# ScalarE reads a shared PSUM bank first, and the planner keeps accesses of one bank apart

## The chip, the cores and the metric

The kernel runs on one core of a Trainium2 chip. Five engines work on it side by side, each through a queue of its own, in order: TensorE (PE, matrix products into PSUM), VectorE (DVE), ScalarE (ACT), GpSimd (POOL) and SyncE (SP), which issues the DMA transfers. PSUM has eight banks of 512 fp32 values for each of 128 partitions; here each bank is one tile. The metric is the device time of one launch in microseconds.

## The reference

Two decoder layers are computed for 512 prompt tokens and 8 x 8 sample tokens (576 in all), model width 1024. Per layer:

```
h = rmsnorm(x); z = h @ w_in                      # rq rk rv rz, aq ak av az, iq ik iw, gr ga
rq, rk = rope(rq), rope(rk)                       # 4 heads of 128: rotary over the whole head
o_r = group_norm(retention(rq, rk, rv, state))    # 4 heads
score = sum_h relu(iq_h . ik) * iw_h              # indexer, 4 heads of 64
o_a = softmax attention of aq over the top-k keys by score (8 query heads, 2 key heads)
m = sigmoid(gr) * ((o_r * silu(rz)) @ w_o_ret) + sigmoid(ga) * ((o_a * silu(az)) @ w_o_att)
x = x + m @ w_out;  x = x + sigmoid(x @ w_ple_gate) * (p @ w_ple_proj)
```

All is fp32. The outputs are the tokens of both sets, the new keys, values and indexer keys, and the retention states.

## The kernel before

The work of a layer is written as some dozens of generators, each of which yields the instructions of one strand: a projection, the evacuation of one PSUM bank, the attention of one pair of heads, the retention of one head. Products are exact to fp32 by splitting each operand in a high and a low fp32r part (`hi`, `lo`; `whi`, `wlo` for weights, `xh`, `xl` for the tokens) and adding three matmuls.

What sets the order of the instructions in the engines' queues is a planner that runs while the program is built (class `Streams`). It keeps a clock for each engine and a log of accesses. For the next instruction of each strand `_ready` finds the time from which it may run: the end of each logged access that overlaps it in partitions **and columns**, where one of the two writes, plus a hop between engines (`HOP`), and a second, safer time with a margin (`MARGIN`, 1.0 for TensorE). `go` takes the strand whose instruction can start first by the safer time, appends that instruction to its engine's queue for good, and advances the clock. All instructions are recorded at line 299 of the kernel (`op.fn(*op.a, **op.k)`), so every row of the profile has that line, and the tiles tell what it is. The semaphores come from the framework, after the planner has fixed the order.

The eight banks are `pm` (three, the projections), `tq` (scores), `ta` (transposes), `oT` (attention output), `tr` and `acc` (retention). A strand takes a bank with `Get`, and gives it back with `K.put` when its last reader has been planned.

Four places read one bank with two engines, and the diff touches them:

- `ropeT` (line 1091): evacuates half of a rotary head from `pm` (32 halves in the program). VectorE multiplies it by the cosine (`d`, in the rows `xl<-pm,rot`), ScalarE copies the two partition halves crosswise into `tb` (`tb<-pm`, 64x288), VectorE multiplies `tb` by the sine and adds.
- `cross_split` (line 743): splits transposed queries from `ta` into high and low parts (`qs<-ta`, `iqs<-ta`), first for partitions 0 to 63, then for 64 to 127.
- `collect` (line 966): adds the crosswise halves of an attention output from `oT`.
- `ret_s` (line 1189): the sample side of a retention head. TensorE writes the sample scores (`tr<-xl 64x64`) and the transposed keys (`tr<-cst,xl 64x128`) into one `tr` bank; VectorE masks the scores (`xh<-tr,cst 64x64`), ScalarE takes the high part of the keys twice (`iqs<-tr`), VectorE the low part twice. Then TensorE writes the head's output into `acc` (`acc<-xh 32x128`, then `acc<-s,xl`).

The prompt side of a head (`ret_p`, line 1142) uses the same two banks: scores into `tr` (masked by `xh<-tr,cst 128x512`), the key transposes into `tr` (`tr<-cst,xl 128x128`, four), the output into `acc`, from which `group_norm` (line 1123) reads statistics with VectorE and then four blocks of columns with ScalarE (`xh<-acc,gs`), and the transposes of the result into `tr` (`tr<-cst,xh 128x128`).

A layer's projections come in the order of `PLAN`: keys, indexer queries, retention values, attention gates `az`, then for each of four heads `rq`, `rk`, `rz`, with the attention queries `aq` between them, then 16 gate units (`gr`, `ga`), which only fill TensorE beside the rest of the attention, then the merge (`pm<-oh,whi`, which needs all strands before it), the output projection and the gates of the layer's end.

Of the kernel before, what the change touches and what calls it, by code (L numbers as in the profile page):

```python
# [23 lines left out]
NS = 64  # L24
# [81 lines left out]
class Op:  # L106
    __slots__ = ("eng", "fn", "a", "k", "name", "outs", "ins", "dur", "form")

    def __init__(self, eng, fn, name, a, k):
        self.eng, self.fn, self.name, self.a, self.k = eng, fn, name, a, k  # L110
        aps = [x for x in list(a) + list(k.values()) if isinstance(x, bass.AP)]
        out = k.get("out", a[0] if a else None)
        acc = k.get("accum_out")
        self.outs = [_box(x) for x in (out, acc) if x is not None]
        self.form = (_val(a[1].partition_size) > 64, min(2, _free(a[1]) - 1 >> 5)) if eng == "PE" else None
        self.ins = [_box(x) for x in aps if x is not out and x is not acc]
        self.dur = _duration(eng, name, out, aps, a, k)
        if eng in ("DVE", "ACT") and len(self.ins) and self.outs[0][1] != self.ins[0][1]:
            self.dur += 0.12
# [78 lines left out]
class Streams:  # L198
# [7 lines left out]
    def __init__(self):  # L206
# [5 lines left out]
        self.count = 0  # L212
        self.form = None

    def spawn(self, gen, prio):
# [39 lines left out]
    def _ready(self, op):  # L255
        t = safe = 0.0
        for boxes, w in ((op.ins, False), (op.outs, True)):
            for name, p0, p1, c0, c1 in boxes:
                for e in self.log.get(name, ()):
                    if (w or e[6]) and e[0] < p1 and p0 < e[1] and e[2] < c1 and c0 < e[3]:  # L260
# [5 lines left out]
                        if r > safe:  # L266
                            safe = r
        return t, safe

    def _note(self, op, end):  # L270
        low = min(self.clock["PE"], self.clock["DVE"], self.clock["ACT"]) - 5.0
        for boxes, w in ((op.ins, False), (op.outs, True)):
# [41 lines left out]
def tile_hybrid_decoder(ctx: ExitStack, tc: tile.TileContext, A, O):  # L314
# [253 lines left out]
    def layer(l, xh, xl, kxb):  # L568
# [174 lines left out]
        def cross_split(dst, ps):  # L743
            d = dst.rearrange("p (a b) t -> p a b t", b=2)
            yield S.activation(d[0:64, :, 0, :], ps[0:64], AF.Copy)
            yield V.tensor_tensor(d[64:128, :, 0, :], ps[0:64], d[0:64, :, 0, :].bitcast(FT), OP.subtract)
            yield S.activation(d[64:128, :, 1, :], ps[64:128], AF.Copy)
            yield V.tensor_tensor(d[0:64, :, 1, :], ps[64:128], d[64:128, :, 1, :].bitcast(FT), OP.subtract)
# [217 lines left out]
        def collect(j, u, oT, done):  # L966
            yield done
            t = yield Get(T2)
            o = t[:, :256]
            for kv in range(2):  # L970
                mine, other = slice(kv * 64, kv * 64 + 64), slice(64 - kv * 64, 128 - kv * 64)
                c = slice(kv * 256, (kv + 1) * 256)
                yield S.activation(o[mine], oT[other, c], AF.Copy)
                yield V.tensor_tensor(o[mine], oT[mine, c], o[mine], OP.add)
            K.put(BANK["oT"], oT)
# [115 lines left out]
        def ropeT(dst, ev, free):  # L1091
            def evac(ps, cs):
# [4 lines left out]
                d = dst[:, cs]  # L1097
                yield V.tensor_tensor(d, ps[:, :TH], cosr[:, cs], OP.mult)
                yield S.activation(tb[0:64], ps[64:128, :TH], AF.Copy)
                yield S.activation(tb[64:128], ps[0:64, :TH], AF.Copy)  # L1100
                K.put(BANK["pm"], ps)
                yield V.tensor_tensor(tb, tb, sinr[:, cs], OP.mult)
# [86 lines left out]
        def ret_s(h, t):  # L1189
# [15 lines left out]
            yield V.memset(ins[:NS, NS:96], 0.0)  # L1205
            yield V.tensor_tensor(ins[:NS, :NS], b[:NS, :NS], con("blk", NS), OP.mult)
            yield S.activation(kh[:NS], b[:NS, 128:256], AF.Copy, scale=g8)
            yield S.activation(kh[NS:], b[:NS, 128:256], AF.Copy, scale=g8)
            for rows in (slice(0, NS), slice(NS, 128)):
                yield V.scalar_tensor_tensor(kl[rows], b[:NS, 128:256], g8, kh[:NS].bitcast(FT), op0=OP.mult,  # L1210
# [415 lines left out]
```

## Time and profile before

| | us |
|---|---|
| timed runs, median (lowest to highest) of 3 | 1113.51 (1112.26 to 1114.78) |
| profiled execution, device time | 1115.49 |
| its span, first to last instruction | 1113.7 |
| TensorE busy in the span | 1084.8 (97%) |
| VectorE / ScalarE busy | 759.1 (68%) / 525.2 (47%) |
[...]

A busy TensorE is read with care: matmuls overlap, and their ends are modelled. Its speed is better read from the distance of their starts, and its losses from the idle time that the waits name. An engine's idle time costs something only where another engine waits for what it does next.

### The profile page before, as it was taken

To read this page: it belongs to the slowest core of one execution; us is meant where nothing else is said; L and a number is where in the kernel's file an instruction comes from. 1 tells how busy PE (TensorE), PEld (TensorE's weight loads), DVE (VectorE), ACT (ScalarE), POOL (GpSimd) and SP (SyncE) were. 2 spreads that over 40 slices of the span, in tenths; PEclk is the share of its full clock that TensorE was granted. 3 is DMA by queue.
4 is the path that set the end of the run, shared out by engine and by line. 5 is a ranking of instruction groups with operands and counts; after the bars stand their busy time and mean duration, and the time that the engine had idled before them with its cause. 6 is when DMAs were issued, how large, how long until landed. Compare 5 with 4: busy or idle time off the path is not lost.

```text
span 1113.7 us, 21594 instructions
## 1 busy us (share of the span) xinstructions
PE 1084.8 (97%) x8426; PEld 1049.9 (94%) x8426; DVE 759.1 (68%) x1979; ACT 525.2 (47%) x1116; POOL 57.4 (5%) x68
## 2 busy tenths in 40 slices
PE   8999899999999999999999998999999999999998
PEld 7989898989999999999999998988989999999998
DVE  6799999976555476534658999998755554764343
ACT  6743264666465343234546333555654655232431
POOL 0100012100000000000010001120000000000000
PEclk9999999999999999999999999999999999999999
DMA  6532221324323364522335221222242233553231
GB/s 199 160 109 74 87 68 69 99 76 127 111 89 118 103 200 156 182 89 97 108 116 163 79 76 58 88 87 98 74 130 102 90 112 131 183 198 121 94 114 48
DMA packets 53112, 124.80 MB, mean 112 GB/s; under 512 B 7442, under 2 KB 19602, under 8 KB 53010
## 3 DMA queue, kind: packets, MB, share of 16 engines
q1 hardware_dynamic: 53010, 123.42, 33.7%
q8 instruction: 66, 1.08, 0.4%
q14 instruction: 36, 0.29, 0.1%
HBM read 103.05 MB, written 20.35 MB: 111 GB/s over the span
## 4 chain that ended last, share of the span: by engine, by line
PE 63%; DVE 28%; ACT 3%; issue 2%; DMA 1%; SPq 1%; POOL 0%; DVEq 0%; ACTq 0%
PE pm L299 53%; DVE xl L299 7%; DVE sm L299 5%; DVE wlo L299 5%; PE oT L299 3%; PE tq L299 3%; PE acc L299 2%; DVE misc L299 2%; DVE silz L299 2%; PE ta L299 2%; PE tr L299 1%; DVE t2k L299 1%; DVE iqs L299 1%; DVE tb L299 1%; DVE qs L299 1%
## 5 line engine op out<-in xcount | busy, mean ns | idle before, releaser
L299 PE MATMUL pm<-xh,whi 128*128 128x288 f32 x1536 | 458.2, 298 | 0.0
L299 PE MATMUL pm<-xl,whi 128*128 128x288 f32 x1536 | 457.1, 298 | 0.0
L299 PE MATMUL pm<-xh,wlo 128*128 128x288 f32 x1536 | 456.8, 297 | 0.0
L299 PEld LDWEIGHTS pm<-xl,whi 128*128 128x128 f32 x1536 | 290.4, 189 | 1.6 <-issue 0.5
L299 PEld LDWEIGHTS pm<-xh,whi 128*128 128x128 f32 x1536 | 290.1, 189 | 0.9
L299 PEld LDWEIGHTS pm<-xh,wlo 128*128 128x128 f32 x1536 | 290.0, 189 | 0.8
L299 ACT ACTIVATE whi<-wst 128x1024 fp32r<-128x1024 f32 (+4 forms) x148 | 150.1, 1016 | 200.3 <-PE pm L299 128.6
L299 DVE TENSOR_TENSOR wlo<-wst,whi 128x1024 fp32r<-128x1024 f32 (+4 forms) x148 | 172.8, 1169 | 82.0 <-ACT whi L299 81.6
L299 PE MATMUL pm<-wlo,xh 128*128 128x256 f32 (+2 forms) x416 | 117.5, 290 | 1.9 <-DVE wlo L299 1.9
L299 PE MATMUL pm<-whi,xh 128*128 128x256 f32 (+2 forms) x416 | 118.2, 291 | 0.0
L299 PE MATMUL pm<-whi,xl 128*128 128x256 f32 (+2 forms) x320 | 93.0, 291 | 0.0
L299 PEld LDWEIGHTS pm<-wlo,xh 128*128 128x128 f32 x416 | 80.1, 193 | 3.5 <-DVE wlo L299 2.4
L299 PEld LDWEIGHTS pm<-whi,xh 128*128 128x128 f32 x416 | 80.1, 193 | 0.7 <-issue 0.4
L299 PE MATMUL pm<-oh,whi 128*128 128x288 f32 x240 | 70.9, 296 | 0.0
L299 PE MATMUL pm<-oh,wlo 128*128 128x288 f32 x240 | 70.9, 295 | 0.0
L299 PE MATMUL pm<-ol,whi 128*128 128x288 f32 x240 | 70.8, 295 | 0.0
L299 ACT ACTIVATE t2k<-t2k,sm 128x256 f32<-128x256 f32 (+3 forms) x102 | 58.7, 583 | 25.2 <-DVE sm L299 21.0
L299 PEld LDWEIGHTS pm<-whi,xl 128*128 128x128 f32 x320 | 61.6, 193 | 0.5 <-issue 0.4
L299 DVE TENSOR_TENSOR misc<-pm,R 128x288 f32<-128x288 f32 x64 | 29.1, 454 | 41.9 <-PE pm L299 41.5
L299 DVE MAX8 sm<-xl 128x8 f32<-128x256 f32 (+2 forms) x96 | 52.4, 549 | 0.8
L299 DVE MATCH_REPLACE8 xl<-sm,xl 128x256 f32<-128x256 f32 (+2 forms) x96 | 51.7, 540 | 0.0
L299 DVE TENSOR_TENSOR ptl<-ta,pth 128x512 fp32r<-128x512 f32 (+1 forms) x48 | 28.7, 598 | 29.8 <-ACT pth L299 29.6
(257 smaller groups left out, 1711.7 us busy)
## 6 DMA issues: line engine op xcount, KB each, us to landing
wst<-in_wa SPq DMA_DIRECT2D x96, 512.0 KB, 3.5
wst<-in_wb SPq DMA_DIRECT2D x16, 512.0 KB, 3.9
wst<-in_wo SPq DMA_DIRECT2D x16, 512.0 KB, 4.0
zgr<-misc SPq DMA_DIRECT2D x16, 288.0 KB, 2.0
zga<-misc SPq DMA_DIRECT2D x16, 288.0 KB, 2.1
misc<-zgr SPq DMA_DIRECT2D x16, 288.0 KB, 2.8
misc<-zga SPq DMA_DIRECT2D x16, 288.0 KB, 4.4
s<-in_ckv SPq DMA_DIRECT2D x32, 128.0 KB, 3.2
```

The costliest lines, as they stand in the source:

```text
L299: op.fn(*op.a, **op.k)
```

## The change

The planner gets a second rule. Each instruction carries the set of PSUM banks that it touches (`banks`), and for each bank the planner notes when each engine's last planned access ends. An instruction may then be planned only after the accesses of all *other* engines to its banks, whichever columns they have, and whether they read or write; the hop between ScalarE and VectorE, which the table does not have, is 0.15. The four places above are written in another order: ScalarE's reads first, then VectorE's.

```diff
--- before.py
+++ after.py
@@ -104,7 +104,7 @@
 
 
 class Op:
-    __slots__ = ("eng", "fn", "a", "k", "name", "outs", "ins", "dur", "form")
+    __slots__ = ("eng", "fn", "a", "k", "name", "outs", "ins", "dur", "form", "banks")
 
     def __init__(self, eng, fn, name, a, k):
         self.eng, self.fn, self.name, self.a, self.k = eng, fn, name, a, k
@@ -112,6 +112,7 @@
         out = k.get("out", a[0] if a else None)
         acc = k.get("accum_out")
         self.outs = [_box(x) for x in (out, acc) if x is not None]
+        self.banks = {x.tensor.name for x in aps if x.space == PSUM}
         self.form = (_val(a[1].partition_size) > 64, min(2, _free(a[1]) - 1 >> 5)) if eng == "PE" else None
         self.ins = [_box(x) for x in aps if x is not out and x is not acc]
         self.dur = _duration(eng, name, out, aps, a, k)
@@ -211,6 +212,7 @@
         self.run = []
         self.count = 0
         self.form = None
+        self.bank = {}
 
     def spawn(self, gen, prio):
         self.count += 1
@@ -265,9 +267,17 @@
                             r += MARGIN.get(op.eng, 0.0)
                         if r > safe:
                             safe = r
+        for name in op.banks:
+            for eng, end in self.bank.get(name, {}).items():
+                if eng != op.eng:
+                    r = end + self.HOP.get((eng, op.eng), 0.15)
+                    t = max(t, r)
+                    safe = max(safe, r + MARGIN.get(op.eng, 0.0))
         return t, safe
 
     def _note(self, op, end):
+        for name in op.banks:
+            self.bank.setdefault(name, {})[op.eng] = end
         low = min(self.clock["PE"], self.clock["DVE"], self.clock["ACT"]) - 5.0
         for boxes, w in ((op.ins, False), (op.outs, True)):
             for name, p0, p1, c0, c1 in boxes:
@@ -743,8 +753,8 @@
         def cross_split(dst, ps):
             d = dst.rearrange("p (a b) t -> p a b t", b=2)
             yield S.activation(d[0:64, :, 0, :], ps[0:64], AF.Copy)
+            yield S.activation(d[64:128, :, 1, :], ps[64:128], AF.Copy)
             yield V.tensor_tensor(d[64:128, :, 0, :], ps[0:64], d[0:64, :, 0, :].bitcast(FT), OP.subtract)
-            yield S.activation(d[64:128, :, 1, :], ps[64:128], AF.Copy)
             yield V.tensor_tensor(d[0:64, :, 1, :], ps[64:128], d[64:128, :, 1, :].bitcast(FT), OP.subtract)
 
         iqt = {}
@@ -967,11 +977,11 @@
             yield done
             t = yield Get(T2)
             o = t[:, :256]
+            mine = [slice(kv * 64, kv * 64 + 64) for kv in range(2)]
             for kv in range(2):
-                mine, other = slice(kv * 64, kv * 64 + 64), slice(64 - kv * 64, 128 - kv * 64)
-                c = slice(kv * 256, (kv + 1) * 256)
-                yield S.activation(o[mine], oT[other, c], AF.Copy)
-                yield V.tensor_tensor(o[mine], oT[mine, c], o[mine], OP.add)
+                yield S.activation(o[mine[kv]], oT[mine[1 - kv], kv * 256:(kv + 1) * 256], AF.Copy)
+            for kv in range(2):
+                yield V.tensor_tensor(o[mine[kv]], oT[mine[kv], kv * 256:(kv + 1) * 256], o[mine[kv]], OP.add)
             K.put(BANK["oT"], oT)
             yield e_az
             z = silz[1][:, 2 * u:2 * u + 2, j * 128:(j + 1) * 128]
@@ -1095,9 +1105,9 @@
                     yield free
                 tb = yield Get(TB)
                 d = dst[:, cs]
-                yield V.tensor_tensor(d, ps[:, :TH], cosr[:, cs], OP.mult)
                 yield S.activation(tb[0:64], ps[64:128, :TH], AF.Copy)
                 yield S.activation(tb[64:128], ps[0:64, :TH], AF.Copy)
+                yield V.tensor_tensor(d, ps[:, :TH], cosr[:, cs], OP.mult)
                 K.put(BANK["pm"], ps)
                 yield V.tensor_tensor(tb, tb, sinr[:, cs], OP.mult)
                 yield V.tensor_tensor(d, d, tb, OP.add)
@@ -1203,9 +1213,9 @@
             ks = yield Get(IQS)
             kh, kl, vh = ks[:, 0], ks[:, 1], ks[:, 2]
             yield V.memset(ins[:NS, NS:96], 0.0)
-            yield V.tensor_tensor(ins[:NS, :NS], b[:NS, :NS], con("blk", NS), OP.mult)
             yield S.activation(kh[:NS], b[:NS, 128:256], AF.Copy, scale=g8)
             yield S.activation(kh[NS:], b[:NS, 128:256], AF.Copy, scale=g8)
+            yield V.tensor_tensor(ins[:NS, :NS], b[:NS, :NS], con("blk", NS), OP.mult)
             for rows in (slice(0, NS), slice(NS, 128)):
                 yield V.scalar_tensor_tensor(kl[rows], b[:NS, 128:256], g8, kh[:NS].bitcast(FT), op0=OP.mult,
                                              op1=OP.subtract)
```

The planner's rule shows in the order of the queues; three places follow, first as they were, then as they are. Names are output tile, then input tiles; a number behind an underscore is the buffer. The line at which the planner records is 309 now.

VectorE, the second and third rotary half of the first head's queries and keys in layer one. `xl<-pm,rot` is the product with the cosine, `tb<-tb,rot` that with the sine. Before:

```order
L299 TENSOR_TENSOR xl<-pm_69,rot 128x288 [waits PE_49]
L299 MATCH_REPLACE xl<-sm_417,xl 128x384 [waits DVE_49]
L299 MAX sm_412<-xl 128x8 [waits DVE_49]
L299 TENSOR_TENSOR wlo_125<-wst_120,whi_122 128x1024 [waits DMAHW7_49,Activation_49]
L299 TENSOR_TENSOR tb_434<-tb_434,rot 128x288 [waits Activation_49]
L299 MAX sm_413<-xl 128x8 [waits DVE_49]
L299 TENSOR_TENSOR xl<-xl,tb_434 128x288 [waits DVE_49]
L299 TENSOR_TENSOR xl<-pm_68,rot 128x288 [waits PE_49]
L299 TENSOR_TENSOR tb_433<-tb_433,rot 128x288 [waits Activation_49]
```

After:

```order
L309 MATCH_REPLACE xl<-sm_412,xl 128x384 [waits DVE_49]
L309 MAX sm_417<-xl 128x8 [waits DVE_49]
L309 TENSOR_TENSOR wlo_125<-wst_120,whi_122 128x1024 [waits DMAHW7_49,PE_49,Activation_49]
L309 TENSOR_TENSOR xl<-pm_69,rot 128x288 [waits Activation_49]
L309 TENSOR_TENSOR tb_434<-tb_434,rot 128x288
L309 MAX sm_414<-xl 128x8 [waits DVE_49]
L309 TENSOR_TENSOR xl<-xl,tb_434 128x288 [waits DVE_49]
L309 MATCH_REPLACE xl<-sm_414,xl 128x384 [waits DVE_49]
L309 TENSOR_TENSOR xl<-pm_68,rot 128x288 [waits PE_49,Activation_49]
L309 TENSOR_TENSOR tb_433<-tb_433,rot 128x288
```

The sine product stands right behind the cosine product, and the wait for ScalarE has moved from the one to the other.

TensorE, the first head of layer two, from the end of the projection that runs beside it. `tr_74<-cst,xl 128x128` are the four key transposes of the prompt side, `acc_75<-xh` and `acc_75<-s` the sample output. Before:

```order
L299 MATMUL pm_70<-wlo_125,xh 128x256
L299 MATMUL tr_74<-cst,xl 128x128 [waits DVE_49]
L299 MATMUL pm_70<-whi_122,xh 128x256
L299 MATMUL pm_70<-whi_122,xl 128x256
L299 MATMUL acc_75<-xh 32x128 x8
L299 MATMUL acc_75<-s_6216,xl 32x128 [waits DMAHW2_49]
L299 MATMUL ta_72<-cst,misc 128x128 x2
L299 MATMUL acc_75<-s_6216,xl 32x128 x7
L299 MATMUL tr_74<-cst,xl 128x128 x3
```

After:

```order
L309 MATMUL pm_70<-whi_122,xh 128x256
L309 MATMUL acc_75<-xh 32x128 [waits DVE_49]
L309 MATMUL acc_75<-xh 32x128 x7
L309 MATMUL acc_75<-s_6216,xl 32x128 [waits DMAHW2_49]
L309 MATMUL acc_75<-s_6216,xl 32x128 x2
L309 MATMUL ta_72<-cst,misc 128x128 [waits DVE_49]
L309 MATMUL ta_72<-cst,misc 128x128
L309 MATMUL acc_75<-s_6216,xl 32x128 x5
L309 MATMUL tr_74<-cst,xl 128x128 x4
```

The four transposes came in two parts, one ahead of the sample output and three behind; now all four stand behind it. Between the sample scores and the first transpose there were 23 rows, and now there are 38.

TensorE, the third head of layer one: `acc_75<-xh` is the first writer of `acc` after the group norm of the prompt side, `tr_74<-cst,xh` are the transposes of the normalised prompt output, `oT` is attention. Before:

```order
L299 MATMUL ta_72<-cst,misc 128x64 [waits DVE_49]
L299 MATMUL ta_72<-cst,misc 128x64
L299 MATMUL oT_73<-ptl_425,vhl 128x256
L299 MATMUL oT_73<-pth_424,vhl 128x256
L299 MATMUL oT_73<-ptl_425,vhl 128x256
L299 MATMUL acc_75<-xh 32x128 [waits Activation_49]
L299 MATMUL acc_75<-xh 32x128 x3
L299 MATMUL tr_74<-cst,xh 128x128 [waits DVE_49]
L299 MATMUL acc_75<-xh 32x128 x4
```

After:

```order
L309 MATMUL pm_69<-xh,whi_121 128x288
L309 MATMUL pm_69<-xl,whi_121 128x288
L309 MATMUL acc_75<-xh 32x128 [waits DVE_49,Activation_49]
L309 MATMUL acc_75<-xh 32x128 x7
L309 MATMUL acc_75<-s_430,xl 32x128 [waits DMAHW4_49]
L309 MATMUL acc_75<-s_430,xl 32x128 x7
L309 MATMUL oT_73<-pth_424,vhl 128x256 [waits Activation_49]
L309 MATMUL tr_74<-cst,xh 128x128 [waits DVE_49]
L309 MATMUL tr_74<-cst,xh 128x128 x3
```

The writer of `acc` has moved behind more projection matmuls (from 24 to 43 rows behind the sample scores of the head), and the transposes into `tr` behind the whole sample output.

## Rows read from the trace of the kernel before

**Rows 1.** The page: busy us, share of the span, instructions, by engine.
```profile
PE 1084.8 (97%) x8426; PEld 1049.9 (94%) x8426; DVE 759.1 (68%) x1979; ACT 525.2 (47%) x1116; POOL 57.4 (5%) x68
```

**Rows 2.** The chain that ended last, its longest pieces: start us, us, what.
```profile
399.19 159.22 PE pm L299 x1200
...
950.18 159.23 PE pm L299 x1200
```

**Rows 3.** Busy time by stage: stage, its length, engines' busy us, PEclk, DMA.
```profile
125.00:160.00 35.00, 31.69 (x257) 29.97 (x256) 33.81 (x118) 17.30 (x41) 5.96 (x6) 0.95 0.25 89
...
645.00:690.00 45.00, 40.45 (x314) 38.15 (x313) 42.51 (x122) 14.80 (x30) 2.02 (x2) 0.96 0.21 71
```

**Rows 4.** Waits of TensorE: us in total, times, longest us.
```profile
PE acc L299 <- ACT xh L299: 5.1, 7, 1.3
PE tr L299 <- DVE xh L299: 3.9, 2, 3.1
PE tr L299 <- DVE iqs L299: 3.6, 4, 2.1
```

**Rows 5.** Timeline around 777 us: start us, us, engine, operation [idle before].
```profile
774.77 0.44 ACT L299 ACTIVATE xh<-acc,gs 128x128 f32<-128x128 f32 x1
...
775.68 0.46 ACT L299 ACTIVATE xh<-acc,gs 128x128 f32<-128x128 f32 x1
...
776.24 0.79 ACT L299 ACTIVATE xh<-acc,gs 128x128 f32<-128x128 f32 x2
...
777.08 0.42 PE L299 MATMUL acc<-xh 64*32 64x128 f32 x8 [1.30 <-ACT xh L299]
```

**Rows 6.** Timeline of TensorE, five other users of the two banks.
```profile
180.19 0.30 PE L299 MATMUL tr<-cst,xh 128*128 128x128 f32 x1 [0.94 <-DVE iqs L299]
...
227.79 0.42 PE L299 MATMUL acc<-xh 64*32 64x128 f32 x8 [1.00 <-ACT xh L299]
...
684.39 0.33 PE L299 MATMUL tr<-cst,xl 128*128 128x128 f32 x1 [2.09 <-DVE iqs L299]
...
736.58 0.42 PE L299 MATMUL acc<-xh 64*32 64x128 f32 x8 [0.84 <-ACT xh L299]
...
812.87 0.31 PE L299 MATMUL acc<-xh 64*32 64x128 f32 x4 [0.89 <-ACT xh L299]
```

**Rows 7.** Busy time by stage, three stretches of 3.42 us with PEclk near 0.5.
```profile
228.86:232.28 3.42, 3.42 (x24) 2.40 (x24) 1.85 (x7) 1.50 (x5) 0.72 (x1) 0.50 0.00 0
686.28:689.70 3.42, 3.42 (x26) 3.02 (x26) 2.38 (x13) 1.39 (x4) 0.00 (x0) 0.51 0.03 5
778.44:781.86 3.42, 3.42 (x28) 2.64 (x19) 1.64 (x7) 0.00 (x0) 0.70 (x1) 0.51 0.00 0
```

**Rows 8.** Timeline of one rotary half, VectorE and ScalarE.
```profile
117.86 0.45 DVE L299 TENSOR_TENSOR xl<-pm,rot 128x288 f32<-128x288 f32 x1
118.40 0.83 ACT L299 ACTIVATE tb<-pm 64x288 f32<-64x288 f32 x2 [2.98 <-DVE xl L299]
119.26 1.06 ACT L299 ACTIVATE whi<-wst 128x1024 fp32r<-128x1024 f32 x1
119.27 0.46 DVE L299 TENSOR_TENSOR tb<-tb,rot 128x288 f32<-128x288 f32 x1 [0.96 <-ACT tb L299]
```

**Rows 9.** Waits of VectorE, 80 to 125 us and 610 to 690 us.
```profile
DVE tb L299 <- ACT tb L299: 1.5, 2, 1.0
...
DVE tb L299 <- ACT tb L299: 0.9, 2, 0.5
```

**Rows 10.** Groups of ScalarE instructions: busy us, mean ns of one, idle before.
```profile
L299 ACT ACTIVATE whi<-wst 128x1024 fp32r<-128x1024 f32 x132 | 139.4, 1057 | 182.1 <-PE pm L299 116.8 <-issue 62.5 <-DMA wst<-in_wb 2.0
...
L299 ACT ACTIVATE tb<-pm 64x288 f32<-64x288 f32 x64 | 26.0, 406 | 32.9 <-DVE xl L299 28.9 <-DVE sm L299 1.8 <-DVE misc L299 1.4
```

**Rows 11.** Timeline of one query split, ScalarE's second read.
```profile
165.43 0.38 ACT L299 ACTIVATE qs<-ta 64x256 fp32r<-64x256 f32 x1 [0.24 <-DVE qs L299]
```

## The prediction

> **What bounds the kernel now.** I read the page's busy times first [rows 1]: TensorE is busy 97% of the span, VectorE 68%, ScalarE less than half. So any gain must be time in which TensorE stands still or runs slowly. The chain of waits tells where that is not the case [rows 2]: its longest piece is 1200 projection matmuls in 159.22 us without a break, 0.133 us each, from the merge of one layer to its gates; the second layer has the same piece from 950.18. There nothing that this change touches is late. What is left is the stretch of each layer in which attention, the indexer and retention run beside the projections (about 25 to 375 us and 573 to 950 us).
>
> The view of the busy times by stage shows that in parts of these stretches a second engine is full [rows 3]: VectorE works 33.81 of 35 us (97%) and 42.51 of 45 us (94%), while TensorE is busy 31.69 and 40.45. The view of waits says what TensorE waits for there [rows 4]: the tile acc for ScalarE's xh (5.1 us in 7 times), the tile tr for VectorE's xh (3.9 us) and for VectorE's iqs (3.6 us).
>
> The timeline shows that the first and the third are of one kind. Around 777 us [rows 5] ScalarE normalises the retention output of one head in four reads of acc: one at 774.77, one at 775.68, two from 776.24. TensorE's next user of acc writes columns 0 to 127 first, which only the read of 774.77 needed; yet it starts at 777.08, when the last read has ended, after 1.30 us of idling. So the program waits for the whole bank, while the planner of the kernel before counts only accesses whose columns overlap, and put the matmul too early in TensorE's queue. TensorE takes its queue in order, so all projection matmuls behind it stand as well. The same shows at 180.19, 227.79, 684.39, 736.58 and 812.87 [rows 6]. At 684.39 the tile is tr: its new user writes the columns that only VectorE's block mask had read, but waits 2.09 us until VectorE's second remainder read of the same bank is through.
>
> [...]
>
> **The change part by part.** *The planner's bank rule.* It adds no instruction to the chip. It moves TensorE's users of acc and tr further back, behind more projection matmuls. The order shows how far. For the first head of the second layer, 23 rows stood between the sample scores (tr from xl, 64x64) and the first of the four key transposes; now it is 38, and 15 x 0.133 = 2.0 us of work cover the 2.09 us wait. For the third head the first user of acc stands 43 rows behind the scores in place of 24 in layer one (19 x 0.133 = 2.5 us against 1.00) and 55 in place of 16 in layer two (5.2 us against 1.30). The second heads go from 27 to 79 rows and from 63 to 83. Only the fourth head of layer two comes nearer, 24 in place of 32, and I leave its 0.89 us standing. The waits of this kind are 0.94 + 1.00 + 2.09 + 0.84 + 0.89 + 1.30 = 7.1 us by rows 5 and 6; without the 0.89 that is 6.2 us. Bounds: 0, if the time comes back elsewhere, and 7.1.
>
> *The clock.* Two of the three slow stretches follow waits of acc that the new order covers well; I count 2 x 1.7 = 3.4 us. Bounds: 0 and 5.1.
>
> *Rotary halves (32, two ScalarE reads each).* Before, VectorE reads pm first, ScalarE's two reads wait for it, and VectorE's product with the sine waits for them. [Rows 8] show one: VectorE's read at 117.86, ScalarE's pair from 118.40 after 2.98 us of idling, then VectorE stands 0.96 us until 119.27. Now ScalarE goes first and both VectorE instructions stand behind it side by side, as the order shows, so one crossing is gone. ScalarE was idle, so its earlier start costs nothing there. In the two stretches that end in TensorE's waits for xh, VectorE lost 1.5 us and 0.9 us in this way [rows 9]. Those waits (3.1 us and 3.9 - 3.1 = 0.8 us, rows 4) are VectorE's backlog, so they shrink by 1.5 and 0.8: 2.3 us. The price of the new wait, VectorE's cosine product behind ScalarE, is not in this trace. From below it is -2.3 us. From above VectorE stands through a whole pair of reads in every half, 32 x 2 x 0.406 = 26 us [rows 10], less the 2.3. I take the lower end, since it is nearer to the row: before the 64 reads ScalarE stood idle for 32.9 us, 28.9 of it for VectorE's own product [rows 10], so it will mostly be early.
>
> *Query split, head collection, sample keys.* The split goes from ScalarE, VectorE, ScalarE, VectorE to two and two. In the trace ScalarE's second read waits 0.24 us for VectorE's first [rows 11], and now VectorE starts a read of 0.38 us later. TensorE's waits in rows 4 do not name this pair, and VectorE has other work queued: I count 0, between -2 and +2 (44 splits, some 0.05 us each). [...]
>
> *What comes back.* Where VectorE is at 94 to 97%, TensorE cannot run ahead of it for long: of the waits there (0.94, 2.09 and 0.84, 3.9 us) I let half return, 2 us. And the whole order is dealt anew (1265 lines of TensorE's queue differ); I allow one new wait of the usual size, 1 us, for each layer: 2 us.
>
> Sum: 6.2 + 3.4 + 2.3 - 2 - 2 = 8 us less. The profiled execution took 1115.49 us (span 1113.7 and 1.8 around it), so 1107.5 by it. It lies 2.0 above the median of the timed runs, 1113.51 (1112.26 to 1114.78), and against that the sum gives **1105.5 us**.
>
> **Rivals.**
> (a) All goes: every wait of the bank kind, all three slow stretches and the rotary waits, and nothing returns: 7.1 + 5.1 + 2.3 = 14.5, so 1099 us. For it: attention now ends closer to the merge, with 96 rows between its last matmul and the first of the merge in place of 143, so the plan gives VectorE and ScalarE some 48 x 0.133 = 6 us more in each layer. Against it: VectorE's load in rows 3.
> (b) All comes back: VectorE is the true bound of the stretches, and TensorE, early by 1 or 2 us, stands at VectorE's next product instead. Then only part of the rotary term is left, 1 us: 1112.5 us. For it rows 3; against it that the last waits, at 777 and 813, have no such load behind them.
> (c) Slower: VectorE, the fuller engine, stands at the head of its queue for ScalarE in the rotary halves. ScalarE's conversion of a weight tile takes 1.06 us [rows 10] and lies between the pairs (rows 8 have one right behind). If in half of the 32 halves VectorE stands through the pair, that is 16 x 0.81 = 13 us less the 2.4 it stood before; the part in the dense stretches, about two thirds or 7 us, reaches TensorE, eats the gain of the bank rule there, and leaves 1113.5 + 7 - 2.3 (the two acc waits at 228 and 777) = 1118 us. It decides from a mean wait of about 0.3 us a half. Against it: ScalarE is the emptier engine. [...]
> (d) The tail: attention ends so late that the merge waits. The 96 rows left are 12.7 us of projections, against some 4 us for the last collection, so it would need 8 us of further delay in each layer; then about 1117 us.
>
> **How the numbers follow.** Forecast (4 to 12 us less) 0.51; (a) 0.18; (b) 0.16; (c) 0.12; (d) 0.03. The forecast alone would have 1101.5 to 1109.5. The range takes (a) and (b) in and leaves (c) and (d) out with the far edge of (a): 1097.5 to 1114.5 us. What this kernel's measurement can tell from no change is about 0.2%, 2.2 us. Faster by more than that: the forecast and (a), 0.69. Within it: (b), 0.16. Slower: (c) and (d), 0.15.
>
> **What would show it.** After the change TensorE's waits of acc for xh and of tr for iqs should fall from 8.7 us to under 4, and fewer than three of the slow clock stretches should follow them. VectorE's sine product should have no wait, and its cosine product little (under 3 us over the 32). The 159.2 us pieces should stay. It is wrong if VectorE's waits for ScalarE's tb grow beyond 8 us, if TensorE's waits for VectorE rise by what those for banks fall, or if the merge's first matmuls wait for the last collection.

## The result and the profile after

The changed kernel takes **1099.16 us** (median; 1098.96 to 1099.43) against 1113.47 (1112.26 to 1114.78) of the kernel before: a ratio of 0.9871, 95% interval [0.9854, 0.9889], or 14.3 us less. The forecast was 8 us less (1105.5, range 1097.5 to 1114.5); the time is that of rival (a), "all goes", 1099. The profiled execution took 1099.24 us with a span of 1097.5, so 16.2 us less span than the profiled one of before.

The page's busy times by engine show how little else moved: the same instructions run, and TensorE fills one more per cent of a shorter span [rows 1].

```profile
PE 1076.7 (98%) x8426; PEld 1044.2 (95%) x8426; DVE 757.6 (69%) x1979; ACT 526.6 (48%) x1116; POOL 63.1 (6%) x68
```

The chain of waits says in which layer the time went (start us, length us, what).

```profile
393.94 159.20 PE pm L309 x1200
...
933.93 159.22 PE pm L309 x1200
```

Against [rows 2] the long projection piece starts 5.25 us earlier in layer one and 16.25 earlier in layer two, so layer two gave 11.0 us of the 16.25. The pieces keep their 159.2 us: nothing behind attention changed.

TensorE's waits (us in total, times, longest us) show the bank kind gone.

```profile
PE tr L309 <- DVE xh L309: 2.8, 2, 1.5
...
PE oT L309 <- ACT pth L309: 1.1, 2, 0.9
PE ta L309 <- DVE qs L309: 0.9, 2, 0.5
...
PE tr L309 <- DVE iqs L309: 0.5, 2, 0.4
...
PE acc L309 <- ACT xh L309: 0.4, 1, 0.4
```

acc for xh and tr for iqs were 5.1 and 3.6 us [rows 4]; now 0.4 and 0.5. The new waits (oT, ta) add up to about 1 us each. All waits of TensorE in this view sum to 15.8 us after and 24.1 before.

The stages of [rows 3] (length, then busy us of PE, PEld, DVE, ACT, POOL; PEclk; DMA) read now:

```profile
125.00:160.00 35.00, 33.30 (x280) 31.50 (x279) 34.82 (x117) 18.75 (x45) 5.74 (x5) 1.00 0.20 73
...
645.00:690.00 45.00, 43.26 (x352) 41.23 (x351) 44.65 (x137) 17.87 (x37) 5.98 (x5) 1.00 0.22 78
```

VectorE was called full at 94 to 97%; it now does 99% (34.82 of 35, 44.65 of 45). So 94 to 97% was not a ceiling. And PEclk is 1.00 in both (over the whole span the mean granted clock went from 0.994 of full speed to 1.000): none of the slow stretches of before is left. There were four of them, the three of [rows 7] and one that the prediction had overlooked (before):

```profile
133.29:136.71 3.42, 3.42 (x18) 3.42 (x18) 3.27 (x14) 1.21 (x4) 1.01 (x1) 0.50 0.01 2
```

The groups of the rotary halves (busy us, mean ns | idle before them):

```profile
L309 ACT ACTIVATE tb<-pm 64x288 f32<-64x288 f32 x64 | 26.0, 406 | 7.0 <-PE pm L309 4.4 <-issue 1.4
...
L309 DVE TENSOR_TENSOR xl<-pm,rot 128x288 f32<-128x288 f32 x32 | 14.3, 446 | 0.8 <-ACT tb L309 0.7
L309 DVE TENSOR_TENSOR tb<-tb,rot 128x288 f32<-128x288 f32 x32 | 14.2, 444 | 0.0
```

VectorE's product with the sine (tb) no longer waits, its product with the cosine (xl) waits 0.7 us over all 32 halves, and ScalarE's 32.9 us of idling in front of its reads [rows 10] have become 7.0.

### The profile page after: what moved, and what is told of

Read it like the earlier page. It is cut to its first block, busy times and chain, and to the rows that moved or that the text cites. A ratio compares the mean times of both kernels' runs of the same rounds, so it can differ in the third digit from the quotient of the medians.

```text
span 1097.5 us, 21646 instructions
## 1 busy us (share of the span) xinstructions
PE 1076.7 (98%) x8426; PEld 1044.2 (95%) x8426; DVE 757.6 (69%) x1979; ACT 526.6 (48%) x1116; POOL 63.1 (6%) x68
## 4 chain that ended last, share of the span: by engine, by line
PE 67%; DVE 25%; issue 3%; DMA 2%; ACT 2%; SPq 1%; POOL 0%; DVEq 0%; POOLq 0%; ACTq 0%
PE pm L309 56%; DVE xl L309 6%; DVE sm L309 5%; DVE wlo L309 3%; PE tq L309 3%; PE oT L309 3%; PE ta L309 2%; DVE misc L309 2%; DVE silz L309 2%; PE acc L309 2%; PE tr L309 2%; DVE qs L309 1%; DVE sc L309 1%; DVE iqs L309 1%; DVE tb L309 1%
## 5 line engine op out<-in xcount | busy, mean ns | idle before, releaser
L309 ACT ACTIVATE t2k<-t2k,sm 128x256 f32<-128x256 f32 (+3 forms) x118 | 66.6, 575 | 46.5 <-DVE sm L309 38.2
L309 DVE MATCH_REPLACE8 xl<-sm,xl 128x384 f32<-128x384 f32 (+2 forms) x96 | 51.6, 538 | 0.0
```

## The experiments

Twelve kernels ran, each timed against the kernel before on the same chip. What they showed is in one table; its last four columns are us, worked out from the traces: "bank" is TensorE's waits of acc for xh and of tr for iqs; "rotary" is VectorE's waits for ScalarE's tb in the 32 halves; "slow" is the time at half clock (PEclk 0.50 to 0.52 in the rows shown) inside the span of the profiled execution; "hole" is the longest stretch, in either layer, with no projection matmul in TensorE's queue around the first gate (explained below; what is below 5 us depends on how near to the gate one looks).

| kernel | orders | rule | us | ratio, 95% interval | bank | rotary | slow | hole |
|---|---|---|---|---|---|---|---|---|
| before | old | none | 1113.5 to 1114.7 | 1 | 8.7 | 6.0 | 13.6 | 2.1 |
| before_rope_inplace (same program) | old | none | 1115.27 | 1.0002 [0.9987, 1.0017] | 8.8 | 6.1 | 3.4 | 2.1 |
| before_orders_inplace (collection only) | old | none | 1116.30 | 1.0011 [0.9996, 1.0026] | 9.4 | 6.0 | 23.9 | 2.1 |
| before_redeal | old | none | 1119.49 | 1.0039 [1.0026, 1.0052] | 10.5 | 6.8 | 10.2 | 1.6 |
| rule_only | old | all | 1107.20 | 0.9935 [0.9921, 0.9949] | 0.4 | 0.9 | 6.8 | 9.4 |
| pe_only | old | TensorE | 1116.81 | 1.0017 [1.0007, 1.0027] | 1.2 | 5.4 | 17.1 | 15.4 |
| pe_no_rope | new, rotary old | TensorE | 1114.38 | 1.0000 [0.9988, 1.0012] | 0.7 | 6.9 | 6.8 | 17.7 |
| swaps_only | new | none | 1104.69 | 0.9906 [0.9888, 0.9923] | 9.2 | 0.7 | 10.2 | 4.0 |
| rule_actdve | new | ScalarE/VectorE | 1113.21 | 0.9994 [0.9981, 1.0006] | 6.9 | 0.6 | 13.7 | 19.9 |
| after_rope_back | new, rotary turned back | all | 1105.24 | 0.9909 [0.9886, 0.9932] | 1.5 | 2.3 | 0 | 6.2 |
| **after** | new | all | **1099.16** | 0.9871 [0.9854, 0.9889] | 0.9 | 0.7 | 0 | 6.6 |
| rule_pe | new | TensorE | **1097.38** | 0.9848 [0.9830, 0.9866] | 0 | 0.2 | 0 | 3.3 |
| after_redeal2 | new | all | 1113.06 | 0.9982 [0.9972, 0.9992] | 0.7 | 0.9 | 10.2 | 24.5 |
| pe_redeal2 | new | TensorE | 1119.72 | 1.0042 [1.0027, 1.0056] | 0.2 | 2.7 | 17.1 | 18.5 |

### Half of the change at a time

The theory (A) was the prediction's: most of the gain is the bank rule, where TensorE is one of the engines, and the clock that comes with it. Rival B: the read orders. Rival C: that the planner knows of the waits between ScalarE and VectorE at one bank (0.24 us in [rows 11]).

**swaps_only**: the new read orders, the rule switched off in `_ready`.

```
-        for name in op.banks:
+        for name in ():
             for eng, end in self.bank.get(name, {}).items():
```

> The four read orders are the new ones (ScalarE first), the planner's bank rule is off. Theory A (the gain is the bank rule where TensorE is one of the two engines: users of acc and tr are planned further back, and the slow clock stretches behind their waits go): only the rotary term is left, about 2 us, so 1110 to 1112 us; TensorE's waits of acc for xh and of tr for iqs stay at 6 us or more together, and at least two slow clock stretches stay. Theory B (the gain is the read order, one crossing between ScalarE and VectorE less): 1099 to 1103 us.

It took 1104.69 us, between what the two theories expected. TensorE's waits of it:

```profile
PE acc L309 <- ACT xh L309: 7.7, 6, 1.6
...
PE tr L309 <- DVE xh L309: 2.6, 2, 1.4
...
PE tr L309 <- DVE iqs L309: 1.5, 1, 1.5
```

The bank waits stand as they were (9.2 us), and still the kernel is 10 us faster than before. A alone does not explain that.

**rule_only**: the whole rule, the four read orders as before (of the four edits to the changed kernel, the rotary one).

```
-                yield S.activation(tb[0:64], ps[64:128, :TH], AF.Copy)
-                yield S.activation(tb[64:128], ps[0:64, :TH], AF.Copy)
                 yield V.tensor_tensor(d, ps[:, :TH], cosr[:, cs], OP.mult)
+                yield S.activation(tb[0:64], ps[64:128, :TH], AF.Copy)
+                yield S.activation(tb[64:128], ps[0:64, :TH], AF.Copy)
...
```

> The planner's bank rule is on, the four places are written in the old order. Theory A: most of the gain, 1100 to 1104 us; acc and tr waits under 2 us, no slow stretch behind them; VectorE's sine products wait 4 us or more as before. Theory B: 1110 to 1114 us.

1107.20 us, again between the two theories (1100 to 1104 and 1110 to 1114). The bank waits are gone (0.4), and so are most of the rotary waits, though VectorE reads first again (VectorE's sine product):

```profile
L309 DVE TENSOR_TENSOR tb<-tb,rot 128x288 f32<-128x288 f32 x32 | 14.3, 446 | 0.9 <-ACT tb L309 0.9
```

More of VectorE's work stands in between: by the trace 154 of its instructions lie between cosine and sine product in the 32 halves, 104 in the kernel before. The likely reason is that the planner now counts ScalarE's reads as late. In these deals, then, the two halves of the change are partly substitutes: alone they gain 7.2 and 10.5 us, together 14.3 and not 17.7. But each of the three kernels is also planned in an order of its own, and the section after this one shows that a new order alone moves the time by more than that difference.

**rule_pe** and **rule_actdve**: all new orders, and the rule for one kind of pair only.

```
-                if eng != op.eng:
+                if eng != op.eng and "PE" in (eng, op.eng):      # rule_pe
+                if eng != op.eng and "PE" not in (eng, op.eng):  # rule_actdve
```

> As the changed kernel, but the bank rule holds only where one of the two engines is TensorE. Theory A: 1098 to 1102 us. Theory C (what counts is that the planner knows ScalarE and VectorE to exclude each other, so that its clocks of these two are true): 1106 to 1112 us.

> As the changed kernel, but the bank rule holds only between ScalarE and VectorE, not where TensorE is one of the two. Theory A: 1107 to 1112 us, with TensorE's acc and tr waits back at 6 us or more. Theory C: 1098 to 1103 us.

rule_pe is the fastest kernel of the study, 1097.38 us; whether it beats the changed kernel (1099.16) the overlapping intervals leave open. rule_actdve (1113.21, just above A's 1107 to 1112) is no faster than before. Read as a table this is A's answer: TensorE's part does it. The next runs show that it must not be read so quickly.

### The same kernels, dealt anew

The planner's order is one deal among many. The rivals R and N say that the deal moves the time by as much as the change does. These runs change one planner number, VectorE's margin, by 0.01 us; neither the rule nor the orders. By the traces some 2600 to 3000 of TensorE's 8426 rows then stand at another place in its queue.

```
-MARGIN = {"DVE": 0.15, "ACT": 0.1, "PE": 1.0}
+MARGIN = {"DVE": 0.16, "ACT": 0.1, "PE": 1.0}
```

In **before_redeal** this is done to the kernel before, in **after_redeal2** to the changed one, in **pe_redeal2** to rule_pe.

> The kernel before with one number of the planner changed (VectorE's margin 0.16 in place of 0.15): neither the bank rule nor the read orders, but TensorE's queue is dealt anew (some 5000 lines differ). Theory A (the two parts of the change make the time): within 3 us of the kernel before, 1110.5 to 1116.5, with waits of acc and tr of the bank kind of 6 to 11 us and two to four slow-clock stretches. Theory R (any re-deal of this order moves the time by several us, and the change drew a good one): more than 4 us away from the kernel before, with the waits of the bank kind as they were.

> The changed kernel with the same number changed (VectorE's margin 0.16), so both parts of the change stand and the order is dealt anew. Theory A: 1096 to 1103 us, no or one slow-clock stretch, acc waits under 1.5 us. Theory R: 1104 to 1112.

> All new read orders, bank rule only where TensorE is one of the two engines, VectorE's margin 0.16 in place of 0.15: the fastest kernel so far, dealt anew. Theory Q (TensorE's part of the rule with the new read orders is better whatever the deal): 1097 to 1103. Theory N (the deal decides by more than the rule): 1106 to 1115, with a slow-clock stretch behind a new wait of TensorE of 1.5 us or more, as in the changed kernel dealt anew (1113).

The kernel before becomes 5 us slower, the changed one 14, and rule_pe 22: from the fastest of the study to the slowest. A and Q gave 1096 to 1103 for the last two and are refuted as to time. R and N point the right way, though the last two came out slower than even their ranges (1104 to 1112 and 1106 to 1115). The mechanism of A, less waiting for banks, holds all the same. The kernel before, dealt anew:

```profile
PE acc L299 <- ACT xh L299: 5.9, 7, 1.2
PE tr L299 <- DVE iqs L299: 4.6, 3, 2.4
```

and the changed one, dealt anew:

```profile
PE ta L309 <- ACT t2k L309: 3.4, 1, 3.4
...
PE tr L309 <- DVE iqs L309: 0.7, 2, 0.4
```

The bank waits come with every deal without the rule (8.7 to 10.5 us) and go with every deal that has its TensorE part (0 to 1.5 us). What the second deal brings is another wait, of 3.4 us, and the timeline around it shows of what kind (after_redeal2, TensorE; start us, us, operation [idle before]):

```profile
250.50 0.30 PE L309 MATMUL tr<-cst,xl 128*64 128x128 f32 x1
254.24 0.90 PE L309 MATMUL ta<-cst,t2k 128*128 128x128 f32 x3 [3.43 <-ACT t2k L309]
```

and at the end of the same hole:

```profile
273.53 0.86 DVE L309 TENSOR_TENSOR qs<-ta,qs 64x256 fp32r<-64x256 f32 x2
...
274.50 0.38 PE L309 MATMUL pm<-xh,whi 128*128 128x288 f32 x1
```

From 250.3 to 274.5 us TensorE's queue holds no projection matmul (pm) at all, only attention's, the indexer's and retention's small ones. One of them stands 3.43 us for ScalarE's t2k, and no filler covers that. The hole ends right behind the last query split (qs). The weights of the next projection are not what is missing, for VectorE has their low part ready 22 us earlier (after_redeal2):

```profile
251.31 1.23 DVE L309 TENSOR_TENSOR wlo<-wst,whi 128x1024 fp32r<-128x1024 f32 x1 [0.30 <-ACT whi L309]
```

The program says what the hole ends with: the planner does not begin the first gate's projection (`gr`, 0) before all of `e_q`, `e_iq`, `e_k` and `e_rr` are set, that is before every query split is planned. When the last retention projection is through before that, nothing is left to fill TensorE. The busy times of the hole's first two parts (after_redeal2):

```profile
250.50:254.30 3.80, 0.37 (x4) 0.17 (x3) 2.89 (x12) 3.76 (x11) 0.00 (x0) 0.95 0.39 120
254.30:264.50 10.20, 9.62 (x78) 7.51 (x79) 4.58 (x20) 3.53 (x12) 0.70 (x1) 0.52 0.45 137
```

TensorE is busy 0.37 of 3.80 us, then the granted clock is at half (0.52) for 10.2 us. In these two parts that costs at most 3.4 + 0.6 + 9.6 / 2 = 8.8 us of the 13.9 between the two deals, an estimate that counts the idle time of both and half of the busy time at half clock. The long projection pieces show that nearly all of the difference arises in this layer. In after_redeal2 they start at:

```profile
406.44 159.22 PE pm L309 x1200
...
947.28 159.24 PE pm L309 x1200
```

Against the changed kernel (393.94 and 933.93) layer one, with the hole, is 12.5 us longer, and layer two, which has none over 4 us, only 0.8. pe_redeal2 has such a hole in both layers; in the second:

```profile
799.60:807.20 7.60, 5.20 (x50) 4.00 (x48) 6.01 (x30) 5.09 (x17) 0.58 (x1) 0.99 0.63 226
807.20:817.40 10.20, 9.08 (x60) 7.28 (x60) 4.62 (x17) 5.31 (x14) 1.12 (x2) 0.50 0.30 97
```

Here too each layer with a hole is 10 to 12 us longer than that of rule_pe (404.75 against 392.49 to the first piece, 549.81 against 539.37 from piece to piece). The first projection behind the hole in layer two starts at 818.08, 0.11 us before the last query split ends:

```profile
817.76 0.43 DVE L309 TENSOR_TENSOR qs<-ta,qs 64x256 fp32r<-64x256 f32 x1
...
818.08 0.40 PE L309 MATMUL pm<-xh,whi 128*128 128x288 f32 x1
```

So the matmul does not wait for the split itself; the condition held it back in the plan. The changed kernel has a hole too, of 6.6 us in layer one, but works through it at full clock (1.00):

```profile
241.60:248.20 6.60, 5.35 (x40) 4.11 (x39) 4.83 (x9) 5.07 (x14) 0.00 (x0) 1.00 0.21 79
```

In the table the hole sorts the kernels better than the bank waits do. All five with a hole over 15 us take 1113 us or more, whatever else they have. Of the others only those of the kernel before are as slow, with old bank waits and old rotary waits together. Of the three deals without any rule none has a hole over 4.0; of the eight with some of it five have one over 15. So the rule seems to bring it, perhaps because it pushes attention's rows back behind projections, and these run out. That is a count over eleven deals, small enough for chance; a run that makes a hole by itself was not made.

When the granted clock falls, the rows do not settle. It stayed full (1.00) through a stretch with 5.35 busy of 6.60 us, and half (0.52 and 0.50) came behind 0.37 of 3.80 and behind 5.20 of 7.60. But half (0.50) also followed 7.66 busy of 9.80 us in pe_no_rope, so the busy share of a whole stretch does not tell when the clock falls.

### The rotary halves

**pe_only** and **pe_no_rope**: the rule of rule_pe with all old orders, and with the rotary order alone as before (the three swapped lines of rule_only's diff).

> Old read orders, bank rule only where TensorE is one of the two engines. With the four kernels run so far this completes a table of read order by rule. Theory A' (read order and TensorE's part of the rule save apart from each other, some 10 and 7 us): 1103 to 1107, acc waits under 1.5, VectorE's tb waits about 1 to 3 us in the stretches where TensorE waits for xh. Rival (the two remove the same stalls): 1097 to 1101, as with the new read orders. Rival C (the rule between ScalarE and VectorE is needed where the old read order has them alternate): 1108 to 1114.

> Rule only where TensorE is one of the two engines, new read orders of the query split, the collection and the sample keys, but the rotary halves read as before (VectorE first). My prediction put the whole worth of the read orders into the rotary halves (2.3 us) and none into the split. Theory of the rotary halves: 1101 to 1106, VectorE's sine product waits for ScalarE's tb again and TensorE waits 2 to 4 us more for VectorE's xh, qs and iqs. Theory of the split (its first read of VectorE stands behind both ScalarE reads and frees the bank sooner): 1097 to 1099, as with all the new orders.

Both are as slow as the kernel before (pe_only even 2 us slower), above all that was expected. VectorE's sine product in pe_no_rope:

```profile
L309 DVE TENSOR_TENSOR tb<-tb,rot 128x288 f32<-128x288 f32 x32 | 14.5, 453 | 6.9 <-ACT tb L309 6.9
```

It waits again, but each of the two also drew a hole (pe_no_rope, the part of it at half clock):

```profile
805.70:812.50 6.80, 6.80 (x53) 5.20 (x52) 2.65 (x9) 3.31 (x9) 0.70 (x1) 0.50 0.23 76
```

So 17 us between pe_no_rope and rule_pe are the rotary order and a new deal together. To part them, the next runs swap reads after planning, so that the queues of TensorE and ScalarE stay as they are, row for row.

**after_rope_back**: the plan is that of the changed kernel; VectorE's cosine product is then issued ahead of ScalarE's first read, 1 to 6 rows earlier in VectorE's queue.

```
-                yield S.activation(tb[0:64], ps[64:128, :TH], AF.Copy)
+                cos = V.tensor_tensor(d, ps[:, :TH], cosr[:, cs], OP.mult)
+                first_read = S.activation(tb[0:64], ps[64:128, :TH], AF.Copy)
+                ahead(first_read, cos)        # issues cos, then first_read
+                yield first_read
                 yield S.activation(tb[64:128], ps[0:64, :TH], AF.Copy)
-                yield V.tensor_tensor(d, ps[:, :TH], cosr[:, cs], OP.mult)
+                yield cos                     # planned here, already issued
```

> The changed kernel with VectorE's cosine product put back ahead of ScalarE's two reads after planning: TensorE's queue is that of the changed kernel row for row, VectorE's product moves ahead by a row or two. Theory T: 1104 to 1109, the sine product waits 4 to 7 us for ScalarE again. Theory P: 1100.5 to 1103. Theory N: 1098 to 1100.5.

1105.24 us: 6.1 us above the changed kernel by the medians, 4.2 by the two ratios (0.9909 less 0.9871, times 1114). That is theory T's range. The two kernels were not timed side by side, and the intervals of the two ratios just touch, so the ratios alone do not exclude the 2.3 us of the prediction. Neither kernel has a slow stretch. Its rows (ScalarE's first reads, VectorE's sine product; L1659 and L1660 are the helper's lines):

```profile
L1660 ACT ACTIVATE tb<-pm 64x288 f32<-64x288 f32 x32 | 13.1, 408 | 41.3 <-DVE xl L1659 41.3
...
L309 DVE TENSOR_TENSOR tb<-tb,rot 128x288 f32<-128x288 f32 x32 | 14.4, 450 | 2.5 <-ACT tb L309 2.3
```

ScalarE stands 41.3 us behind VectorE's product. VectorE's own wait is only 2.3 us, below the 4 to 7 expected, yet TensorE loses more:

```profile
PE tr L309 <- DVE xh L309: 3.6, 2, 2.1
PE oT L309 <- ACT pth L309: 1.6, 4, 0.5
PE ta L309 <- ACT t2k L309: 1.2, 4, 0.5
PE acc L309 <- ACT xh L309: 1.0, 2, 0.7
```

Against the rows of the changed kernel that is 0.8 more for VectorE's xh, 0.5 for ScalarE's pth, 0.6 for its xh and 1.2 for its t2k, for which the changed kernel shows no wait. Since TensorE's queue is the same, its delay can also be followed row by row through the two traces: 0.5 us at the start, 2.9 from 260 to 550 us, 6.0 from 760 us on, so 5.5 us arise on the way. It rises in steps of 0.2 to 0.8 us, nearly all at rows that wait for t2k, pth or xh, with a few smaller steps back. One of them, first in the changed kernel, then in after_rope_back:

```profile
749.47 0.38 PE L309 MATMUL acc<-xh 128*128 128x128 f32 x2
...
755.52 0.49 PE L309 MATMUL acc<-xh 128*128 128x128 f32 x2 [0.66 <-ACT xh L309]
```

So here ScalarE, standing 41.3 us in the rotary halves, was late for the attention and retention tiles queued behind them. The prediction called ScalarE idle and its start free. One thing this run does not part: its plan was made for the other order, and a planner that knows of VectorE's first read may lose less.

**before_rope_inplace** and **before_orders_inplace** were to do the reverse on the kernel before.

```
+                then(second_read, cos)        # was to issue cos behind second_read
```

> The kernel before with the rotary halves' read order swapped after planning: the plan is that of the kernel before and every engine's queue holds the same rows in the same order; only who waits for whom in the 32 rotary halves is turned round (VectorE's cosine product now waits for ScalarE's two reads, its sine product no longer does). So nothing is dealt anew. Theory T (the rotary waits of VectorE are the larger part of the gain, 6.0 us of them in the kernel before): 1105 to 1109 us, sine product's wait 0, cosine product's under 3. Theory P (the prediction's size, 2.3 us): 1110.5 to 1113. Theory N (the swap is worth nothing by itself, and what separates the kernels is how the order was dealt): 1113 to 1116. My rival (c): above 1116.

> The kernel before with all four read orders swapped after planning (rotary halves, query split, collection, sample keys), no bank rule, TensorE's queue row for row that of the kernel before. By the prediction (split, collection and keys at 0): within 1.5 us of the run with the rotary halves alone. Rival (the split's VectorE reads, 44 of them, free VectorE's or the bank's time too): 3 to 6 us below it. Second rival (the split's first VectorE read now stands behind both ScalarE reads and holds VectorE up): 2 to 4 us above it.

Neither did what its expectation says. The name `then` is taken by another function inside the kernel, so the call had no effect: the first run is the kernel before once more, and in the second only the head collection is swapped, by lines written out. The sine product of the first shows it:

```profile
L299 DVE TENSOR_TENSOR tb<-tb,rot 128x288 f32<-128x288 f32 x32 | 14.5, 452 | 6.1 <-ACT tb L299 6.1
```

What they are good for: a repeat of the same program gives a ratio of 1.0002, and the collection's swap, without a new deal, changes nothing that can be measured (1.0011 [0.9996, 1.0026]). What the rotary swap does in the order of the kernel before, and the split and the sample keys in any fixed order, stays open.

## Why the prediction was right, and where it was not

Sign and range held, and so did each sign that the prediction named: bank waits under 4 us, fewer than three slow stretches, no wait of the sine product, no wait at the merge. The size was short by 6.3 us, and by its own steps for these reasons.

- **Bank waits: right.** Forecast 6.2 us of 8.7 gone, bounds 0 and 7.1; measured 8.7 to 0.9 in this deal, and at 1.5 us or less in every deal with the rule's TensorE part. The fourth head of layer two (0.89 us), left standing because its row came nearer, has gone too. The row counts behind this came from a listing that puts equal rows together: by the traces the first transpose of layer two's first head went from 22 to 64 matmuls behind the scores, not from 23 to 38, and that fourth head came nearer from 52 to 40, not from 32 to 24. The cover is there all the same: without the wait 3.0 us of work lay between scores and transpose before, and 6.2 after.
- **"What comes back": wrong.** 2 us were to return in the dense stretches and 2 in new waits. All of TensorE's listed waits fell by 8.3 us (24.1 to 15.8), so net nothing came back. The premise, VectorE full at 94 to 97%, failed: it went to 99%. Of the 1.2 and 2.5 us that it stood in the two stages of [rows 3], it had waited 0.6 and 1.2 us for ScalarE and 1.0 us for TensorE's acc; none of these waits is left. In other deals far more came back than 4 us. The term is not small and steady but a draw, and that this deal drew nothing back is luck.
- **Rotary halves: right direction, too small, and only part of the mechanism.** 2.3 us forecast, 4 to 6 measured. The forecast counted VectorE's waits in two stretches, and took them off TensorE's waits for xh. Those fell from 3.9 to 2.8 us, by 1.1, and one of the two grew. What was left out is ScalarE's standing (41.3 us with the old order in this deal), which delayed what was queued behind it (TensorE's waits for t2k, pth and xh of ScalarE grew by 1.2, 0.5 and 0.6 us).
- **Clock: about right, for a reason that I did not have.** No run shows the 1.7 us a stretch of the sum; it was my estimate, half of the 3.42 us at a PEclk of 0.50 to 0.51 in [rows 7]. Four stretches went, not two, at that price 4 x 1.7 = 6.8 us in the profiled execution. But the kernel before, run 29 times beside after_rope_back, shows that they cost less than 1.7 us each: 8 runs at a mean clock of 0.998 have a mean span of 1111.3 us, 4 at 0.993 one of 1113.5, and a straight line through all 29 gives 0.6 us of span for each us of lost clock, some 1.0 us a stretch. That the engines that TensorE waits for catch up meanwhile is a likely reason, not a shown one. By that line some 3 us of the 14.3 are the clock (the mean clock goes from 0.995 to 0.999, which is 4.4 us of it). That is near the 3.4 of the sum because two errors cancel, too few stretches at too high a price.
- **Split, collection, sample keys: 0.** Borne out for the collection alone.
- **The rivals.** (a) gives the time, 1099, and its events: all bank waits, all slow stretches, nothing back. Its prices are not those measured (the clock less, the rotary halves more), so the equal time is in part luck. (b) fell because TensorE's waits for VectorE did not take the place of the bank waits (xh 3.9 to 2.8), though VectorE is now busy 99% in the two stages of [rows 3]. (c) fell: VectorE's cosine product waits 0.7 us in all, far from the 0.3 us a half from which (c) decides. (d), the tail, had 0.03, and its kin is what makes the slow deals: I looked for the first work that waits for attention at the merge, 96 rows on, while the gates are held back for the last query split much earlier. The 96 rows hold for layer one alone; in layer two they are 48, so that the tail was nearer there than its price says. That its 1117 us lies among the deals with such holes (1113 to 1120) is chance, since it was worked out for another place.

What is shown and what is not: the rotary order is worth 4 to 6 us in the changed kernel's fixed TensorE order, and the bank waits go by the rule. How the other 8 to 10 us divide between the rule, the other read orders and the luck of the deal is not settled. Over the second deal the change is still worth 1119.49 - 1113.06 = 6.4 us, less than half of the first. The long pieces tell which part held: from piece to piece layer two is 11.0 us shorter by the change in the first deal and 10.2 in the second (551.01 in before_redeal, 540.84 in after_redeal2), while layer one is 5.2 us shorter in the first and 3.0 longer in the second, where it has the hole.

## What to carry to other kernels

Where a planner orders the work, measure a change in more than one deal before you believe its size: one number of the planner, moved by a hundredth, gives the control. Test a change of a local order with the rest of the order held fixed. Compare layer by layer, since one layer can keep a gain that the other loses. And when a rule moves waiting rows back behind filler work, look for the place where the filler runs out: the first work that depends on the rows moved back.

## What the runs showed that was not expected

- A planner number moved by 0.01 us moved the times of three programs by 5, 14 and 22 us, up to 2%.
- Executions of the changed kernel lie within 0.5 us of each other, those of the kernel before within 9 us (1111.8 to 1121.0 in one set of 29), and with the same program the slow stretches differ from run to run: 13.6 us at half clock in one profiled execution, 3.4 in another. The two fastest kernels, without a slow stretch, are the steadiest too (0.5 us each, over four executions).
- TensorE stood 1.5 us for xh in the changed kernel and kept its full clock (125 to 160 us, PEclk 1.00 above); 1.00 us at 227.79 in the kernel before [rows 6] was followed by half clock (0.50). The length of the last stop alone does not tell.
